# Row sums of squared differences: a new last piece, an early end of the tile context, and another assignment of blocks to partitions

## The chip, the core and the metric

The kernel runs on one core of a Trainium2 chip. A core has five engines that run side by side: TensorE (PE), VectorE (DVE), ScalarE (ACT), GpSimd (POOL) and SyncE (SP), and sixteen DMA engines that move data between the device's memory (HBM) and the core's memory (SBUF, 128 partitions). The metric is the device time of one execution in microseconds (us), lower is better. The time before is the median of nine runs.

## What is computed

```python
batch, dim = 1024, 4096
x = np.random.randn(batch, dim).astype(np.float32)
y = np.random.randn(batch, dim).astype(np.float32)

def reference(x, y, axis):          # axis = -1
    return np.sum((x - y) ** 2, axis=axis).astype(np.float32)
```

Two inputs of 16.8 MB are read once, and 1024 floats are written. There is nothing to reuse, and no matrix product.

## The kernel before

The 1024 rows are cut into 128 blocks of eight consecutive rows, one block to a partition: partition p holds rows 8p to 8p+7, a run of N = 8 x 4096 = 32768 columns. So every step of the kernel is about a range of columns of that run, in all 128 partitions at once. D is 4096, the length of a row; "row r" below means the r-th row of every block.

The run is loaded in pieces, listed by their widths in `xw` and `yw` (lines 78 and 79), large ones first and small ones at the end. A piece of x goes to the buffer X, one of y to Y. Both buffers hold H = 6 D columns, so the last two rows of a block come to lie where rows 0 and 1 lay. The y piece of 736 columns that ends row 3 is left out of its place (`late`, lines 80 to 82) and loaded second to last, and the last 352 columns of row 7 come last (line 94). The order is worked out from `ys`: each y piece is preceded by the x pieces that it needs (lines 117 to 123). All loads and the store are issued by SyncE, on one queue; each load has a semaphore of its own, which reaches 16 when it has landed.

The first two loads are put ahead of the barrier with which every program starts (`prog.early`, line 128); the next two, which fill the buffers, follow. The rest waits until squares of row 0 and row 1 are done (lines 223 to 230), because it overwrites these rows.

For each y piece, in the order of `ys`, VectorE waits for the load (`wait_loaded`), and subtracts in place, in parts that end at row ends (`sub`, line 172). ScalarE waits for the difference, squares it and sums it up along the columns into one number per partition (`square`, line 178). A row that has one part only gets its sum in `results` at once; a row in several parts has its partial sums in `parts`. There are three such rows. Row 6 is added up by VectorE (lines 231 to 241). Row 3 is completed by ScalarE, which adds its two partial sums with an Identity activation (lines 216 to 222). Row 7 ends on VectorE: it adds the partial sums so far into `head` (line 196), and one fused instruction (line 202) squares the last 352 differences, sums them and adds `head`.

SyncE then waits for both engines and stores the 128 x 8 results (lines 243 to 246), and waits for the store. `Program` writes all this into the program's first block, ahead of its branch, and takes the tile context's own bookkeeping off meanwhile (lines 16 to 22 and 42 to 50). The tile context closes at the end of the `with` statement in the launching code (line 278 of the profile): a barrier of all engines, GpSimd's clearing of the semaphores, and another barrier.

Of the kernel before, what the change touches and what calls it, by code (L numbers as in the profile page):

```python
# [8 lines left out]
class Program:  # L9
# [4 lines left out]


    def __init__(self, nc, tc):
        self.nc, self.hook = nc, tc.instruction_hook
        self.here = nc.cur_bb.bb.instructions
        self.entry = nc.main_func.blocks[0].instructions
        nc.remove_inst_callback(self.hook)  # L20
        self.lower, nc._always_lower_symbolic_ap = nc._always_lower_symbolic_ap, False
        self.before = len(self.here)

    def _take(self):
        taken = self.here[self.before :]
        del self.here[self.before :]
        return taken

    def _put(self, where):
        self.entry[where:where] = self._take()  # L30

    def early(self, engine):

        self._put(
            next(
                n
                for n, i in enumerate(self.entry)
                if i.engine == engine and str(i.opcode) == "Drain"
            )
        )  # L40

    def close(self):

        self._put(
            next(
                n for n, i in enumerate(self.entry) if str(i.opcode) == "UnconditionalBranch"
            )
        )
        self.nc._always_lower_symbolic_ap = self.lower
        self.nc.push_inst_callback(self.hook)  # L50


def kernel(tc, x, y, axis, out):
    nc = tc.nc
    P = nc.NUM_PARTITIONS
    F32 = mybir.dt.float32
    Square = mybir.ActivationFunctionType.Square
    Identity = mybir.ActivationFunctionType.Identity
    mult, add = mybir.AluOpType.mult, mybir.AluOpType.add

    B, D = x.shape
    R = B // P
    N = R * D


    xv = x.rearrange("(p r) d -> p (r d)", p=P)
    yv = y.rearrange("(p r) d -> p (r d)", p=P)
    ov = out.rearrange("(p r) -> p r", p=P)


    H = 6 * D
# [2 lines left out]
    results = nc.alloc_sbuf_tensor("results", [P, R], F32).ap()  # L74

    xw = [16384, 8192, 3072, 2688, 1312, 768, 352]
    yw = [15648, 8192, 3072, 2688, 1312, 768]
    late, last = 736, 352  # L80
    LATE = 3
    cut = (LATE + 1) * D - late
    assert sum(xw) == N and sum(yw) == N - late - last
# [4 lines left out]
    ys, c = [], 0  # L88
    for w in yw:
        ys.append((c, c + w))  # L90
        c += w
        if c == cut:
            c += late
    ys += [(cut, cut + late), (N - last, N)]

    diffs = tc.alloc_semaphore("diffs")
    acts = tc.alloc_semaphore("acts")
    sums = tc.alloc_semaphore("sums")
    stored = tc.alloc_semaphore("stored")
    n = dict(diffs=0, acts=0, sums=0)  # L100

    prog = Program(nc, tc)

    def home(c0, c1):
        h0 = c0 % H
        return slice(h0, h0 + c1 - c0)
# [3 lines left out]
    freed = []  # L110

    def load(landed, src, dst, name, c0, c1):
        sem = tc.alloc_semaphore("%s%d" % (name, len(landed)))
        nc.sync.dma_start(out=dst[:, home(c0, c1)], in_=src[:, c0:c1]).then_inc(sem, 16)  # L114
        landed.append(((c0, c1), sem))

    order = []
# [8 lines left out]
    for _ in range(2):  # L126
        load(*todo.pop(0))
    prog.early(mybir.EngineType.SP)
    while todo and todo[0][5] <= H:
        load(*todo.pop(0))  # L130


    row_parts = [[] for _ in range(R)]
    for c0, c1 in ys:
        while c0 < c1:
            e = min(c1, (c0 // D + 1) * D)
            row_parts[c0 // D].append((c0, e))
            c0 = e
    parts, where = None, {}
    total = sum(len(p) for p in row_parts if len(p) > 1)  # L140
    parts = nc.alloc_sbuf_tensor("parts", [P, total], F32).ap()
    head = nc.alloc_sbuf_tensor("head", [P, 1], F32).ap()
    k = 0
    for r, p in enumerate(row_parts):
        for piece in p:
# [2 lines left out]
    first = {}  # L148
# [6 lines left out]
    def parts_of(r, m):  # L155
        return parts[:, first[r] : first[r] + m]
# [3 lines left out]
    def wait_loaded(c1, ysem):  # L160

        waits = []
        while seen_x[0] < len(xs) and xs[seen_x[0]][0] < c1:
            waits.append(seen_x[0])
            seen_x[0] += 1
        nc.vector.wait_ge(ysem, 16)
        for k in waits:
            nc.vector.wait_ge(landed_x[k][1], 16)

    def sub(c0, c1):  # L170
        a = X[:, home(c0, c1)]
        nc.vector.tensor_sub(out=a, in0=a, in1=Y[:, home(c0, c1)]).then_inc(diffs, 1)  # L172
        n["diffs"] += 1

    def square(c0, c1, acc):
        a = X[:, home(c0, c1)]
        nc.scalar.wait_ge(diffs, n["diffs"])
        nc.scalar.activation(out=a, in_=a, func=Square, accum_out=acc).then_inc(acts, 1)  # L178
        n["acts"] += 1

    squared = {}
    reuse = []
    for j, (c0, c1) in enumerate(ys):
        final, tail = j == len(ys) - 1, j == len(ys) - 2
        wait_loaded(c1, landed_y[j][1])
        pieces = []
        while c0 < c1:
            e = min(c1, (c0 // D + 1) * D)
            pieces.append((c0, e))
            c0 = e  # L190
        for piece in pieces:
            sub(*piece)
            r = piece[0] // D
            if final:
                nc.vector.wait_ge(acts, squared[row_parts[r][-2]])
                nc.vector.tensor_reduce(  # L196
                    out=head, in_=parts_of(r, len(row_parts[r]) - 1), axis=mybir.AxisListType.X, op=add
                ).then_inc(sums, 1)
                n["sums"] += 1
                nc.vector.wait_ge(sums, n["sums"])  # L200
                nc.vector.wait_ge(diffs, n["diffs"])
                nc.vector.tensor_tensor_reduce(  # L202
                    out=Y[:, home(*piece)],
                    in0=X[:, home(*piece)],
                    in1=X[:, home(*piece)],
                    scale=1.0,
                    scalar=head,
                    op0=mult,
                    op1=add,
                    accum_out=results[:, r : r + 1],  # L210
                ).then_inc(sums, 1)
                n["sums"] += 1
                continue
            square(*piece, where[piece])
            squared[piece] = n["acts"]
            if tail:
                a, b = parts_of(r, 1), parts[:, first[r] + 1 : first[r] + 2]
                nc.scalar.wait_ge(acts, n["acts"])
                nc.scalar.activation(  # L219
                    out=results[:, r : r + 1], in_=b, func=Identity, bias=a  # L220
                ).then_inc(acts, 1)
                n["acts"] += 1
            if r in (0, 1):

                nc.sync.wait_ge(acts, n["acts"])
                while todo and todo[0][5] <= H + (r + 1) * D:
                    load(*todo.pop(0))
                if r == 1:
                    while todo:
                        load(*todo.pop(0))  # L230
        if j == len(ys) - 4:

            r = 6
            nc.vector.wait_ge(acts, squared[row_parts[r][-1]])
            nc.vector.tensor_reduce(  # L235
                out=results[:, r : r + 1],
                in_=parts_of(r, len(row_parts[r])),
                axis=mybir.AxisListType.X,
                op=add,
            ).then_inc(sums, 1)  # L240
            n["sums"] += 1

    nc.sync.wait_ge(sums, n["sums"])
    nc.sync.wait_ge(acts, n["acts"])
    nc.sync.dma_start(out=ov, in_=results).then_inc(stored, 16)
    nc.sync.wait_ge(stored, 16)
    prog.close()


# [33 lines left out]
```

## Time and profile before

| What | us |
|---|---|
| Median of nine runs | 86.02 |
| Their lowest and highest | 85.86, 86.43 |
| The profiled execution's own time | 86.43 |
| Its span, from the first to the last instruction of the kernel | 84.6 |
| VectorE busy | 36.3 (43%) |
| ScalarE busy | 31.7 (37%) |
| GpSimd busy | 0.2 |
| DMA: data moved, mean rate | 33.56 MB, 397 GB/s |
| First subtraction starts | 40.46 |
| Store issued | 82.26 |

The span is what the profile's times count in, from 0; the execution's own time also has what the runtime does around the kernel. VectorE and ScalarE are idle until 40.46, because the first pieces, half of all columns, land together. The row of busy tenths of the DMA engines, with 40 slices for the span, has nines and eights nearly throughout up to slice 38, and nothing in the last slice: what is at the end is not loading.

### The profile page before, as it was taken

Reading aid. Unit: us, or ns where it says so; the run is one execution under the profiler, and the core shown is the slowest. Engines: PE = TensorE matmul, PEld = TensorE weight load, DVE = VectorE, ACT = ScalarE, POOL = GpSimd, SP = SyncE. Lnnn points to the kernel's source line nnn. Section 1 sums busy time; section 2 is a strip of 40 time slices with the busy share of each in tenths; the row PEclk is TensorE's granted clock in tenths of the full one; section 3 lists DMA queues with packets and bytes.
Section 4 is the critical chain, followed back from the end, with each engine's and each line's share of the span. In section 5 each row is a group of like instructions: output and inputs, shape, how many; then the busy total and the mean of one; then the engine's idle time right before and its main releaser. Section 6 shows DMA issues by size and latency. Waiting matters only on the chain.

```text
span 84.6 us, 110 instructions
## 1 busy us (share of the span) xinstructions
DVE 36.3 (43%) x17; ACT 31.7 (37%) x26; POOL 0.2 (0%) x4
## 2 busy tenths in 40 slices
DVE  0000000000000000000899999990699999099870
ACT  4100000000000000000007979799404979996980
POOL 0000000000000000000000000000000000000000
DMA  9559999996699999995988997997999999999800
GB/s 496 248 248 496 496 496 496 496 465 268 266 444 473 473 473 473 473 473 248 480 372 387 496 480 325 434 480 298 412 430 412 431 432 437 402 417 411 323 1 2
DMA packets 2304, 33.56 MB, mean 397 GB/s; under 512 B 384, under 2 KB 640, under 8 KB 1280
## 3 DMA queue, kind: packets, MB, share of 16 engines
q1 hardware_dynamic: 2304, 33.56, 93.9%
HBM read 33.55 MB, written 0.00 MB: 396 GB/s over the span
## 4 chain that ended last, share of the span: by engine, by line
DMA 72%; DVE 14%; ACT 10%; SPq 1%; issue 0%
DMA Y<-in_y_dram 72%; DVE X L172 14%; ACT X L178 10%; SPq L114 1%; ACT results L219 0%
## 5 line engine op out<-in xcount | busy, mean ns | idle before, releaser
L172 DVE TENSOR_TENSOR X<-X,Y 128x4096 f32<-128x4096 f32 (+8 forms) x13 | 35.6, 2781 | 45.8 <-DMA Y<-in_y_dram 45.8
L178 ACT ACTIVATE X<-X 128x4096 f32<-128x4096 f32 (+7 forms) x12 | 29.4, 2452 | 49.2 <-DVE X L172 49.2
L178 ACT ACTIVATION_READ_ACCUMULATOR X<-X 128x1 f32 x12 | 2.2, 187 | 0.0
L178 ACT ACT_TABLE_LOAD x1 | 1.3, 1283 | 1.3 <-PEq L264 1.3
L202 DVE CUSTOM_DVE_ANT_0 Y<-X,head 128x352 f32<-128x352 f32 x1 | 0.6, 584 | 0.1
L219 ACT ACTIVATE results<-parts 128x1 f32<-128x1 f32 x1 | 0.3, 294 | 0.0
L196 DVE TENSOR_REDUCE head<-parts 128x1 f32<-128x3 f32 x1 | 0.1, 150 | 0.0
L235 DVE TENSOR_REDUCE results<-parts 128x1 f32<-128x2 f32 x1 | 0.1, 147 | 0.0
L264 POOL MEMSET const-bfloat16-1.0<- 128x1 bf16 x1 | 0.1, 102 | 0.0
L264 POOL MEMSET const-uint8-127<- 128x1 uint8 x1 | 0.1, 102 | 0.0
L264 POOL MEMSET const-float32-0.0<- 128x1 f32 x1 | 0.1, 99 | 0.2 <-issue 0.2
L264 POOL MEMSET const-float32-1.0<- 128x1 f32 x1 | 0.1, 99 | 0.0
L202 DVE DVE_READ_ACCUMULATOR2_ANT results<- 128x1 f32 x1 | 0.1, 82 | 0.0
## 6 DMA issues: line engine op xcount, KB each, us to landing
Y<-in_y_dram SPq DMA_DIRECT2D x1, 7824.0 KB, 40.0
X<-in_x_dram SPq DMA_DIRECT2D x1, 4096.0 KB, 48.9
Y<-in_y_dram SPq DMA_DIRECT2D x1, 4096.0 KB, 58.4
X<-in_x_dram SPq DMA_DIRECT2D x1, 1536.0 KB, 15.2
Y<-in_y_dram SPq DMA_DIRECT2D x1, 1536.0 KB, 18.5
X<-in_x_dram SPq DMA_DIRECT2D x1, 1344.0 KB, 17.8
Y<-in_y_dram SPq DMA_DIRECT2D x1, 1344.0 KB, 20.6
X<-in_x_dram SPq DMA_DIRECT2D x1, 656.0 KB, 21.8
```

What stands on the lines that cost most here:

```text
L114: nc.sync.dma_start(out=dst[:, home(c0, c1)], in_=src[:, c0:c1]).then_inc(sem, 16)
L172: nc.vector.tensor_sub(out=a, in0=a, in1=Y[:, home(c0, c1)]).then_inc(diffs, 1)
L178: nc.scalar.activation(out=a, in_=a, func=Square, accum_out=acc).then_inc(acts, 1)
L196: nc.vector.tensor_reduce(out=head, in_=parts_of(r, len(row_parts[r]) - 1), axis=mybir.AxisListType.X, op=add).then_inc(sums, 1)
L202: nc.vector.tensor_tensor_reduce(out=Y[:, home(*piece)], in0=X[:, home(*piece)], in1=X[:, home(*piece)], scale=1.0, scalar=head, op0=mult, ...
L219: nc.scalar.activation(out=results[:, r : r + 1], in_=b, func=Identity, bias=a).then_inc(acts, 1)
L235: nc.vector.tensor_reduce(out=results[:, r : r + 1], in_=parts_of(r, len(row_parts[r])), axis=mybir.AxisListType.X, op=add,).then_inc(sums, 1)
L264: nc = _bacc.Bacc("TRN2", target_bir_lowering=False, num_devices=1)
```

## The change

It has three parts.

The pieces. The widths are others. The late piece of row 3 of y is 160 columns in place of 736 and now comes last of all; the last piece of row 7 is 288 columns and comes second to last. So the fused instruction now completes row 3, with that row's one earlier partial sum, and row 7 is summed up behind it by `complete(7)`, as row 6 is by `complete(6)`. The `head` sum and the Identity activation are gone. There are 6 pieces of x in place of 7, and 9 of y in place of 8. A piece of x can now span two pieces of y.

The tile context. It is closed and compiled at the beginning of `Program.__init__`, so that its barriers stand ahead of the body. The body, but for the first two loads, stands behind the branch and behind these barriers. Behind the body GpSimd waits for the store and clears the semaphores, and no engine waits for another.

The blocks. Partition 8e+i takes block 16i+e, in x, in y and in the result. In memory the source is a pattern of 16 x 8 blocks; partitions 8e to 8e+7 hold blocks e, 16+e, 32+e and so on, each 2 MB behind the one before.

```diff
     def __init__(self, nc, tc):
-        self.nc, self.hook = nc, tc.instruction_hook
+        self.nc = nc
+        tc.close()
+        tc.compile()
         self.here = nc.cur_bb.bb.instructions
         self.entry = nc.main_func.blocks[0].instructions
-        nc.remove_inst_callback(self.hook)
-        self.lower, nc._always_lower_symbolic_ap = nc._always_lower_symbolic_ap, False
         self.before = len(self.here)
...
-    def close(self):
-
-        self._put(
-            next(
-                n for n, i in enumerate(self.entry) if str(i.opcode) == "UnconditionalBranch"
-            )
-        )
-        self.nc._always_lower_symbolic_ap = self.lower
-        self.nc.push_inst_callback(self.hook)
+    def close(self, sem, value):
+
+        self.nc.gpsimd.wait_ge(sem, value)
+        self.nc.clear_and_free_semaphores(self.sems)
...
-    xv = x.rearrange("(p r) d -> p (r d)", p=P)
-    yv = y.rearrange("(p r) d -> p (r d)", p=P)
-    ov = out.rearrange("(p r) -> p r", p=P)
+    G = 8
+    xv = x.rearrange("(i e r) d -> e i (r d)", i=G, r=R)
+    yv = y.rearrange("(i e r) d -> e i (r d)", i=G, r=R)
+    ov = out.rearrange("(i e r) -> e i r", i=G, r=R)
...
-    xw = [16384, 8192, 3072, 2688, 1312, 768, 352]
-    yw = [15648, 8192, 3072, 2688, 1312, 768]
-    late, last = 736, 352
+    xw = [16384, 8192, 5568, 1824, 512, 288]
+    yw = [16224, 8192, 2656, 2912, 928, 896, 512]
+    late, last = 160, 288
...
-    ys += [(cut, cut + late), (N - last, N)]
+    ys += [(N - last, N), (cut, cut + late)]
...
+    def complete(r):
+        nc.vector.wait_ge(acts, squared[row_parts[r][-1]])
+        nc.vector.tensor_reduce(
+            out=results[:, r : r + 1],
+            in_=parts_of(r, len(row_parts[r])),
+            axis=mybir.AxisListType.X,
+            op=add,
+        ).then_inc(sums, 1)
+        n["sums"] += 1
...
             if final:
-                nc.vector.wait_ge(acts, squared[row_parts[r][-2]])
-                nc.vector.tensor_reduce(
-                    out=head, in_=parts_of(r, len(row_parts[r]) - 1), axis=mybir.AxisListType.X, op=add
-                ).then_inc(sums, 1)
-                n["sums"] += 1
-                nc.vector.wait_ge(sums, n["sums"])
                 nc.vector.wait_ge(diffs, n["diffs"])
                 nc.vector.tensor_tensor_reduce(
...
-                    scalar=head,
+                    scalar=parts_of(r, 1),
...
-            if tail:
-                a, b = parts_of(r, 1), parts[:, first[r] + 1 : first[r] + 2]
-                nc.scalar.wait_ge(acts, n["acts"])
-                nc.scalar.activation(
-                    out=results[:, r : r + 1], in_=b, func=Identity, bias=a
-                ).then_inc(acts, 1)
-                n["acts"] += 1
...
+        if j == 4:
+            complete(6)
+    complete(7)
 
     nc.sync.wait_ge(sums, n["sums"])
-    nc.sync.wait_ge(acts, n["acts"])
     nc.sync.dma_start(out=ov, in_=results).then_inc(stored, 16)
-    nc.sync.wait_ge(stored, 16)
-    prog.close()
+    prog.close(stored, 16)
```

More of the change, by code (lines that the diff above doesn't have):

```diff
@@ L16, in __init__, with semaphore, early @@
     def __init__(self, nc, tc):
-        self.nc, self.hook = nc, tc.instruction_hook
+        self.nc = nc
+        tc.close()
+        tc.compile()
         self.here = nc.cur_bb.bb.instructions
         self.entry = nc.main_func.blocks[0].instructions
-        nc.remove_inst_callback(self.hook)
-        self.lower, nc._always_lower_symbolic_ap = nc._always_lower_symbolic_ap, False
         self.before = len(self.here)
-    def _take(self):
+        self.sems = []
+    def semaphore(self, name):
+        self.sems.append(self.nc.alloc_semaphore(name))
+        return self.sems[-1]
+    def early(self, engine):
         taken = self.here[self.before :]
         del self.here[self.before :]
[L27 to L32, printed above, removed]
-        self._put(
-            next(
-                n
-                for n, i in enumerate(self.entry)
-                if i.engine == engine and str(i.opcode) == "Drain"
-            )
-        )
-    def close(self):
-        self._put(
-            next(
-                n for n, i in enumerate(self.entry) if str(i.opcode) == "UnconditionalBranch"
-            )
-        )
-        self.nc._always_lower_symbolic_ap = self.lower
-        self.nc.push_inst_callback(self.hook)
+        where = next(
+            n
+            for n, i in enumerate(self.entry)
+            if i.engine == engine and str(i.opcode) == "Drain"
+        )
+        self.entry[where:where] = taken
+    def close(self, sem, value):
+        self.nc.gpsimd.wait_ge(sem, value)
+        self.nc.clear_and_free_semaphores(self.sems)
 def kernel(tc, x, y, axis, out):
@@ L57 @@
     Square = mybir.ActivationFunctionType.Square
-    Identity = mybir.ActivationFunctionType.Identity
     mult, add = mybir.AluOpType.mult, mybir.AluOpType.add
@@ L93 @@
             c += late
-    ys += [(cut, cut + late), (N - last, N)]
[L96 to L99, printed above, removed]
+    ys += [(N - last, N), (cut, cut + late)]
+    prog = Program(nc, tc)
+    diffs = prog.semaphore("diffs")
+    acts = prog.semaphore("acts")
+    sums = prog.semaphore("sums")
+    stored = prog.semaphore("stored")
     n = dict(diffs=0, acts=0, sums=0)
-    prog = Program(nc, tc)
     def home(c0, c1):
@@ L112, in load @@
     def load(landed, src, dst, name, c0, c1):
-        sem = tc.alloc_semaphore("%s%d" % (name, len(landed)))
-        nc.sync.dma_start(out=dst[:, home(c0, c1)], in_=src[:, c0:c1]).then_inc(sem, 16)
+        sem = prog.semaphore("%s%d" % (name, len(landed)))
+        nc.sync.dma_start(out=dst[:, home(c0, c1)], in_=src[:, :, c0:c1]).then_inc(sem, 16)
         landed.append(((c0, c1), sem))
@@ L141 @@
     parts = nc.alloc_sbuf_tensor("parts", [P, total], F32).ap()
-    head = nc.alloc_sbuf_tensor("head", [P, 1], F32).ap()
     k = 0
@@ L181 @@
     squared = {}
-    reuse = []
+    def complete(r):
[7 more added lines that the diff above has]
+        n["sums"] += 1
     for j, (c0, c1) in enumerate(ys):
-        final, tail = j == len(ys) - 1, j == len(ys) - 2
+        final = j == len(ys) - 1
         wait_loaded(c1, landed_y[j][1])
@@ L230 @@
                         load(*todo.pop(0))
[L231 to L241, printed above, removed]
+        if j == 4:
+            complete(6)
+    complete(7)
     nc.sync.wait_ge(sums, n["sums"])
-    nc.sync.wait_ge(acts, n["acts"])
     nc.sync.dma_start(out=ov, in_=results).then_inc(stored, 16)
-    nc.sync.wait_ge(stored, 16)
-    prog.close()
+    prog.close(stored, 16)
 _INS = ['x', 'y', 'axis']
```

## The prediction

> **What bounds the kernel now.** I read the chain that ended last first, then the stretches by time, then the last 10 us instruction by instruction, then the rows of the kernel's last line. The page's chain:
>
> ```profile
> DMA 72%; DVE 14%; ACT 10%; SPq 1%; issue 0%
> DMA Y<-in_y_dram 72%; DVE X L172 14%; ACT X L178 10%; SPq L114 1%; ACT results L219 0%
> ```
>
> Loading takes 72% of the span. Is the loading at a limit? The answer by stretches (columns: stretch, its length, busy us of VectorE, ScalarE, GpSimd, clock, DMA share, GB/s):
>
> ```profile
> 22.00:40.40 18.40, 0.00 (x0) 0.00 (x0) 0.00 (x0) 1.00 0.95 409
> 40.40:50.20 9.80, 9.74 (x3) 4.66 (x3) 0.00 (x0) 1.00 0.99 428
> 50.20:60.10 9.90, 6.93 (x3) 9.27 (x6) 0.00 (x0) 1.00 0.98 410
> 60.10:67.50 7.40, 7.40 (x2) 3.14 (x3) 0.00 (x0) 1.00 1.01 430
> ```
>
> The engines are busy 95 to 101% from start to end; a slice's GB/s jumps with packets that are counted whole, so the rate is better had from landings, in the page's list of issues:
>
> ```profile
> Y<-in_y_dram SPq DMA_DIRECT2D x1, 7824.0 KB, 40.0
> X<-in_x_dram SPq DMA_DIRECT2D x1, 4096.0 KB, 48.9
> X<-in_x_dram SPq DMA_DIRECT2D x1, 22.0
> ```
>
> The first x piece (64 KB in each of 128 partitions, 8.39 MB) lands at 22.0; y's first, issued at 0.42, at 40.4: 7824 KB in 18.4 us is 435 GB/s. At that rate 8.39 MB need 19.3 us, so 2.7 us of the first 22.0 are start-up. The last y piece is issued at 61.88 and lands 19.0 later, at 80.88. All 33.55 MB at 435 are 77.1 us, so 1.1 us are lost in the rest. From the last landing on, loading no longer counts:
>
> ```profile
> 77.08 1.68 ACT X L178 x2
> 78.76 0.00 issue
> 78.77 3.09 ACT X L178 x6
> 81.86 0.02 issue
> 81.88 0.29 ACT results L219
> ```
>
> This is the end of the chain in order of time: ScalarE squares without a gap from 77.08, ends 1.0 us behind the last landing, and the store is issued at 82.26. It lands 1.4 later, at 83.67. What comes then is 0.93 us up to 84.6, and the rows of the last line show it (operation, count, duration, first and last start):
>
> ```profile
> L278 POOLq EVENT_SEMAPHORE  x4: 17/17/17, 83.9 to 84.5; - x4
> L278 POOLq DRAIN  x3: 34/41/88, 1.2 to 84.4; - x3
> L278 SPq EVENT_SEMAPHORE  x2: 17/17/17, 84.1 to 84.6; - x2
> L278 SPq COMPARE_BRANCH  x1: 33/33/33, 83.7 to 83.7; - x1
> L278 POOLq EVENT_SEMAPHORE_RANGE_CLEAR  x1: 138/138/138, 84.2 to 84.2; - x1
> ```
>
> SyncE sees the store (83.7), a barrier of all engines runs (83.9 to 84.1), GpSimd clears the semaphores (84.2), and a second barrier runs (84.5 to 84.6). So the bounds, in order: 80.9 us of loading, 1.4 of tail, 1.4 of store, 0.9 of closing.
>
> [...]
>
> **The change part by part.**
>
> *Closing.* Two barriers go from the end to the start. At the start they stand ahead of the second x and y pieces (issued at 1.26 and 1.64). The closing pass at the end costs about 0.4 us per barrier (83.9 to 84.1 plus drains; 84.2 to 84.6), so these issues come some 0.5 to 1 us later; their engines are busy with the first two pieces until 40.4, which hides it, and ScalarE's table load with them. At the end GpSimd alone waits for the store. Nothing is queued behind that wait but its drain and the clear[...]. Cost: wake-up about 0.05, drain 0.1 (the row has 34 to 88 ns), clear 0.14, so 0.28 in place of 0.93: minus 0.65. Bounds: minus 0.9[...]; minus 0.3, if GpSimd's way out is slow.
>
> *Loads.* 15 before (7 x, 8 y), 15 after (6 x, 9 y), 128 packets each, the same bytes: the fixed costs per transfer cancel. y's first piece grows by 576 columns, 0.68 us at 435 GB/s, so subtraction starts at 41.1, and the second square, which now releases all later loads (x's third piece reaches into row 1's place), ends at 53.65 in place of 52.97. The queue holds work until 60.04 + 0.68, so 7 us of cover; eleven issues at 0.33 to 0.44 us are under 5 us. [...]an issue waits (3.1 us, in before), which was harmless 16 us ahead of the need and still is some 9 ahead. Cost 0.
>
> *Tail.* The rows by shape give VectorE 4420 ns for 4096 and 526 for 352 columns, so 1.04 ns a column + 0.16; ScalarE 3617 for 4096 and 817 for 736, 0.833 + 0.20. Before, 5600 columns remain behind y's fourth piece, which lands at 73.99: 6.89 us, 1.23 ns a column. After, 5408 remain: 6.65, so its counterpart (2912 wide) lands at 74.23. Subtractions of 1440 and 1472: 1.66 + 1.69, less 0.08 overlap, to 77.52. ScalarE is free by then (2656 from 73.6 takes 2.42, 1440 takes 1.40, to 77.45). From 77.55: 1472, 928, 896, 512, 288 at 1.43 + 0.98 + 0.95 + 0.63 + 0.44 = 4.43, to 81.98. Each of these is subtracted in time: 896 by 79.87 for 79.96, 512 by 80.7 for 80.9, 288 by 81.16 for 81.5. The accumulator's read adds 0.10, to 82.08. VectorE meanwhile: 160 subtracted by 81.39, the fused square-and-sum (584 ns for 352, so 0.38) and its read to 81.86; it is done first. Then row 7's reduction, 0.15 and two wake-ups of 0.03: store issue at 82.29, against 82.26. So the shorter last piece is worth nothing, as ScalarE sets the end: the Identity step (0.29) is replaced by wake-up and reduction. I take 0; bounds minus 0.25 and plus 0.3, since ScalarE's chain hangs on y's fourth piece within 0.1 us.
>
> *Store.* 128 pieces of 32 B as before[...] it took 1.4 with neighbours. I take 1.4; bounds minus 0.1, plus 0.3.
>
> *Block order.* Same packets, same partitions; what differs is which 128 KB block each engine reads at one moment[...]. [...] Bound below: start-up down from 2.7 by 0.5, and the stretch at 410 GB/s raised to 428 (0.4 us): minus 0.9. Above: see the slow rival. I take 0.
>
> Sum: minus 0.65. Against the profiled execution, 86.43 - 0.65 = 85.78; that one was the slowest of nine runs, 0.41 above their median, and the parts do not hang on it, so against the median 86.02 - 0.65 = 85.37.
>
> **Rivals.** (1) *The block order also helps*, at start-up and in the 50 to 60 us stretch: 85.37 - 0.9 = 84.5. For: 2.7 us of start-up, and a stretch of 410 with the same packets. Against: that stretch is also when SyncE issues eight loads, which stays. (2) *The closing saves nothing*: [...] 86.0. Against: the two barriers are serial work in the rows shown. (3) *Slower: the sixteen transfer engines collide in the new order*[...] in every load. If the rate of the slow stretch, 410 in place of the mean 420 (33.55 MB over 79.9 us), held throughout, loading would take 81.8, plus 1.9: 87.25. [...]half rate, plus some 75 us: 160. It decides from a loss of 0.65 us in 79.9, 0.8% of the rate. [...]
>
> **How the numbers follow.** Forecast 0.57, (1) 0.17, (2) 0.05, (3) 0.21. Forecast and (1) are faster: 0.74. (2) is the same within 0.2% (0.17 us, about what a measurement tells from no change): 0.05. (3) is slower: 0.21. The forecast's own range is 84.9 to 85.9 by the bounds of closing, tail and store; the range goes down to 84.4 for (1) and up to 87.0, which takes in the milder half of (3) and leaves its rest, about 0.12, and a little of (1) out.
>
> **What would show it.** Closing: the span ends 0.2 to 0.4 after the store's landing, with no barrier rows. Tail: ScalarE gapless from 77.5, the reduction of row 7 last before the store, issue at 82.2 to 82.4. Loads: last landing at 80.9 within 0.2, y's first at 41.1. Wrong, if the last landing moves by over 0.4 us either way (block order), or if the span shrinks by 0.65 and the time does not.

## The result, and the profile after

The changed kernel takes 165.67 us (median of ten runs, 164.14 to 166.38), against 86.02: 1.922 times as long, 95% interval 1.918 to 1.926. The profiled execution took 164.87, its span is 163.0, so 1.87 us lie outside the span, as the 1.83 before (86.43 less 84.6).

The page's parts 1, 3 and 4 of the changed kernel:

```profile
DVE 36.4 (22%) x18; ACT 32.2 (20%) x27; POOL 0.2 (0%) x4
...
q1 hardware_dynamic: 2304, 33.56, 97.2%
HBM read 33.55 MB, written 0.00 MB: 206 GB/s over the span
...
DMA X<-in_x_dram 27%; DMA Y<-in_y_dram 23%; SPq L110 16%; DVE X L167 6%; ACT X L173 2%; DVE Y L201 0%; DVE results L180 0%; DVEq L163 0%; SPq L217 0%; DVE results L201 0%
```

VectorE and ScalarE work about as long as before (36.3 and 31.7 us then). The packets (2304) are as many and the bytes the same. The DMA engines are busy 97.2% of a span that is nearly twice as long: they don't wait, each packet takes longer. One of 64 KB takes 5.11 us in the trace (the median of 128), where it took 2.42. In the chain a further quarter of the span has no name; by the stretches below it is loading too. The 16% at L110 are load issues of SyncE, the longest in the chain of 15.13 us (0.54 to 0.65 each for the first four). They are harmless, as those of 3.10 and 3.30 us were before: in the third stretch below, where they stand, the DMA engines are busy 99% of the time.

The page's list of issues (KB each, us from issue to landing):

```profile
Y<-in_y_dram SPq DMA_DIRECT2D x1, 8112.0 KB, 82.7
X<-in_x_dram SPq DMA_DIRECT2D x1, 4096.0 KB, 100.7
...
X<-in_x_dram SPq DMA_DIRECT2D x1, 43.4
out_dram<-results SPq DMA_DIRECT2D x1, 4.0 KB, 1.8
```

The first x piece (third row) lands at 43.4, where it took 22.0 before. The first y piece, issued at 0.69, lands at 83.4: 8.31 MB in 40.0 us are 208 GB/s, where it was 435. The answer by stretches, between these landings and the next ones, shows that nothing else has to run for this (stretch, its length, busy us of VectorE, ScalarE and GpSimd, clock, DMA share, GB/s):

```profile
43.40:83.40 40.00, 0.03 (x1) 0.00 (x0) 0.00 (x0) 1.00 0.94 195
83.40:103.30 19.90, 17.24 (x4) 13.76 (x7) 0.00 (x0) 1.00 1.01 211
103.30:123.30 20.00, 0.01 (x1) 0.95 (x2) 0.00 (x0) 1.00 0.99 207
```

With both compute engines all but idle (first and third row) or both busy (second), loading runs at half its former rate. It does so nearly to the end; only behind 150 us, where the pieces are small, does it rise, to 251 GB/s from 150 to 159 us. The closing did what was foreseen. The rows of GpSimd's last line:

```profile
L46 POOLq DRAIN  x1: 88/88/88, 162.8 to 162.8; - x1
L46 POOLq EVENT_SEMAPHORE_RANGE_CLEAR  x1: 138/138/138, 162.9 to 162.9; - x1
```

The store is issued at 160.93 and lands 1.8 later, at 162.7; the span ends 0.3 behind that, where it was 0.9.

### The profile page after: what moved, and what is told of

The parts are those of the page before. It is cut to its first block, busy times and chain, and to the rows that moved or that the text cites. A ratio compares the mean times of both kernels' runs of the same rounds, so it can differ in the third digit from the quotient of the medians.

```text
span 163.0 us, 109 instructions
## 1 busy us (share of the span) xinstructions
DVE 36.4 (22%) x18; ACT 32.2 (20%) x27; POOL 0.2 (0%) x4
## 2 busy tenths in 40 slices
DMA packets 2304, 33.56 MB, mean 206 GB/s; under 512 B 384, under 2 KB 768, under 8 KB 1408
## 3 DMA queue, kind: packets, MB, share of 16 engines
q1 hardware_dynamic: 2304, 33.56, 97.2%
## 4 chain that ended last, share of the span: by engine, by line
DMA 50%; another core or an unknown queue 25%; SPq 16%; DVE 6%; ACT 2%; issue 0%; DVEq 0%
DMA X<-in_x_dram 27%; DMA Y<-in_y_dram 23%; SPq L110 16%; DVE X L167 6%; ACT X L173 2%; DVE Y L201 0%; DVE results L180 0%; DVEq L163 0%; SPq L217 0%; DVE results L201 0%
## 5 line engine op out<-in xcount | busy, mean ns | idle before, releaser
L167 DVE TENSOR_TENSOR X<-X,Y 128x4096 f32<-128x4096 f32 (+9 forms) x14 | 35.8, 2594 | 124.5 <-DMA Y<-in_y_dram 124.3
L173 ACT ACTIVATE X<-X 128x4096 f32<-128x4096 f32 (+8 forms) x13 | 29.8, 2292 | 125.9 <-DVE X L167 125.8
```

## The experiments

### Is it the blocks? Taken out, and alone

`old_blocks` is the changed kernel with the assignment of before:

```diff
-    xv = x.rearrange("(i e r) d -> e i (r d)", i=G, r=R)
+    xv = x.rearrange("(p r) d -> p (r d)", p=P)
```

and so for y and the result; the index in the load follows. Two theories of the loss are put to the test from here on: H seeks it in the addresses that are read in HBM, P in the partitions that are written side by side in SBUF.

> The changed kernel with the assignment of blocks of before: partition p holds block p, source pattern 128 rows. Everything else as changed. Theory P[...] and theory H (HBM: sixteen engines that read blocks 128 KB apart collide in HBM) expect the same: the loss is gone, loading ends at 80.9, the closing gain of 0.65 us stays, 85.4 us (85.0 to 85.8).

Measured: 85.32 us (85.22 to 85.43), ratio to before 0.992 (0.991 to 0.994). This version is faster than both kernels. `blocks_alone` is the reverse, the kernel of before with these lines of the change alone.

> The kernel of before with the new assignment of blocks alone (partition 8e+i takes block 16i+e). P and H expect the whole loss: 64 KB packets at some 5.1 us, 165 to 167 us. If it were under 160, part of the loss would come from the new pieces or the closing.

Measured: 162.05, one execution, 3 us under what was expected. Without the assignment the whole loss is gone, and by itself it brings 76 us of it. Why the complete change is 3.6 us slower than that is open.

### HBM or SBUF: patterns in which the two part

The change alters two things at once: which addresses a load reads side by side, and into entries of how many partitions its pattern is divided. `blocks_64x2` and, later, `blocks_32x4` use the same formula with other factors, each in one execution. In 64 x 2 each eight partitions read 512 KB behind the eight before them, in 16 x 8 128 KB. Shown against `blocks_alone`:

```diff
-    G = 8
+    G = 2        # blocks_32x4: 4
```

> The kernel of before with a source pattern of 64 x 2 blocks: partition 2e+i takes block 64i+e. [...] P: 160 to 170 us, as with 16 x 8. H: 86 to 90 us.

Measured: 87.19. `lead128_pitch` keeps 128 partitions as the leading dimension and moves the addresses:

```diff
-    xv = x.rearrange("(p r) d -> p (r d)", p=P)
+    J = 4
...
+    xv = x.rearrange("(j p r) d -> p j (r d)", j=J, p=P)
```

and so for y and the result; a load that crosses a quarter becomes two.

> The kernel of before with a source pattern of 128 rows, in which neighbouring partitions are 32 KB apart (each partition takes two rows from each quarter of the batch), so that partitions four apart,[...] are 128 KB apart in HBM. Two loads are cut in two at the quarters, and the store is in pieces of 8 B. P: 86 to 88.5 us, loading at 420 GB/s or more. H: over 120 us.

Measured: 88.05, the store landing 3.3 us after its issue in place of 1.4. So H failed its own test. P failed in the form in which I had put it: it foresaw 160 to 170 for 64 x 2, which runs at full rate. Two narrower theories were left: P2, that the loss needs entries of eight partitions, and H2, that it needs sixteen streams inside 2 MB. `lead16_step7` has the form 16 x 8 at other addresses; it reads 113 of the 128 blocks, 15 of them twice (not 16, as the text below has it), so its sums are not those of the reference:

```diff
-        nc.sync.dma_start(out=dst[:, home(c0, c1)], in_=src[:, c0:c1]).then_inc(sem, 16)
+        nc.sync.dma_start(
+            out=dst[:, home(c0, c1)],
+            in_=bass.AP(src.tensor, c0, [[7 * N, 16], [N, 8], [1, c1 - c0]]),
+        ).then_inc(sem, 16)
```

> The kernel of before with a source pattern of 16 x 8 whose outer step is 7 blocks and whose inner step is 1 block: partition 8e+i takes block 7e+i. This leaves 16 blocks out and reads others twice; the bytes moved are the same. Sixteen streams are then 896 KB apart, much as in the kernel of before. Theory P2[...]: 160 us or more. Theory H2 (HBM: sixteen streams inside one window of 2 MB collide; neither 64 x 2 nor the 128-row pattern had that): 86 to 88 us.

Measured: 165.69, as slow as the change, with entries 896 KB apart in place of 128.

> The kernel of before with a source pattern of 32 x 4: partition 4e+i takes block 32i+e. P2[...]: 87 us. [...] H2: the streams lie 128 or 256 KB apart in windows of 1 to 4 MB, so anything from 87 to 160 us.

Measured: 86.72. Here are the issues of these two for the first y piece, with the same size, `lead16_step7` first:

```profile
Y<-in_y_dram SPq DMA_DIRECT2D x1, 7824.0 KB, 81.8
```

```profile
Y<-in_y_dram SPq DMA_DIRECT2D x1, 7824.0 KB, 39.9
```

The form of the pattern decides, not the addresses: 16 entries of 8 partitions are slow at either spacing, 32 of 4 and 64 of 2 are fast, with 128 KB from entry to entry as in the change. H2 is out.

### How many engines move how much

Under P2 my estimate was that four engines, on 32 partitions at a time, carry as much as eight on 64: a quarter of 435 GB/s is 109, and four engines at 64 KB in 2.42 us each are 108. Loads were cut into halves or quarters of the partitions, with the pattern 8 x 8 or 4 x 8 in each part:

```diff
+        for q in range(Q):     # half_8x8: Q = 2, quarter_4x8: Q = 4
+            nc.sync.dma_start(
+                out=dst[q * P // Q : (q + 1) * P // Q, home(c0, c1)],
+                in_=src[q, :, :, c0:c1],
+            ).then_inc(sem, 16)
```

> The kernel of before with each load cut into two halves of 64 partitions, each with a source pattern of 8 x 8, so that eight engines work[...]. P2: [...]109 GB/s: 64 KB packets at 5.1 us, loading 308 us, 310 to 325 us in all. H2: at half the demand there are no collisions, 64 KB packets at 2.42 us, loading 155 us, 160 to 175 us in all.

> Each load cut into four quarters of 32 partitions with a source pattern of 4 x 8, so that four engines work[...]. P2: 64 KB packets at 2.42 us, four times 27 GB/s, loading 309 us, 310 to 330 us in all: no longer than with eight engines in the halves. If instead each engine is slow by itself in such a pattern: packets at 5.1 us, 620 us.

Measured: 308.27, just under the range of P2, and 322.40, one execution each. The queue's line and the rate below it on the two pages, `half_8x8` first (packets, MB, share of 16 engines):

```profile
q1 hardware_dynamic: 2304, 33.56, 49.1%
HBM read 33.55 MB, written 0.00 MB: 109 GB/s over the span
```

```profile
q1 hardware_dynamic: 2304, 33.56, 24.5%
HBM read 33.55 MB, written 0.00 MB: 105 GB/s over the span
```

The share says that eight engines (half of sixteen) were busy throughout in the one, and four in the other, with the same number of packets of the same sizes. Eight engines moved 109 GB/s, four 105. So four of them, on 32 partitions at a time, run at 26 GB/s each, and eight on 64 at 14, about half of that. It is no matter of an engine being slow in such a pattern, and none of what HBM gives, which was 435 before.

### The destination alone

`step4_2x8` and `step8_2x8` differ in the destination partitions only. A load has two entries of eight partitions; the second entry lies 32 partitions behind the first in `step4_2x8`, 64 in `step8_2x8`. Two engines work (the DMA share is 0.12 to 0.13, two of sixteen):

```diff
     def mine(q):
-        return slice(q, q + 121, 8)                                        # step8_2x8
+        return slice(q // 4 * 64 + q % 4, q // 4 * 64 + q % 4 + 61, 4)     # step4_2x8
```

> The kernel of before with each load cut into eight of 16 partitions, source pattern 2 x 8, so that two engines work[...] (the 16 partitions lie four apart). Source addresses are those of the run beside it, step8_2x8; only the destination partitions differ. [...]27 GB/s, loading 1230 us or more. If it isn't a matter of the destination: as step8_2x8.

> As step4_2x8, with the same source addresses, but the 16 partitions of a load lie eight apart[...]. [...]54 GB/s, loading 617 us, 620 to 680 us in all, half of step4_2x8. If it isn't a matter of the destination: the same time as step4_2x8.

Measured: 658.98 and 635.08, one execution each. The second is as expected; the first is not the 1230 that I had worked out. The stretches from the start (the last two figures are DMA share and GB/s), `step4_2x8` first:

```profile
0.00:40.00 40.00, 0.00 (x0) 0.00 (x0) 0.20 (x4) 1.00 0.12 29
40.00:80.00 40.00, 0.00 (x0) 0.00 (x0) 0.00 (x0) 1.00 0.13 48
80.00:120.00 40.00, 0.00 (x0) 0.00 (x0) 0.00 (x0) 1.00 0.12 52
120.00:160.00 40.00, 0.00 (x0) 0.21 (x1) 0.00 (x0) 1.00 0.13 56
```

```profile
0.00:40.00 40.00, 0.00 (x0) 0.00 (x0) 0.20 (x4) 1.00 0.12 52
40.00:80.00 40.00, 0.00 (x0) 0.00 (x0) 0.00 (x0) 1.00 0.13 56
80.00:120.00 40.00, 0.00 (x0) 0.00 (x0) 0.00 (x0) 1.00 0.12 52
```

With entries 32 partitions apart, two engines begin at 29 GB/s, about the rate of one (26 in `quarter_4x8`), busy all the time; with entries 64 apart, they begin at 52. So the destination alone costs them about half of their rate. But the loss dissolves: in the next stretches the first run moves 48, 52 and 56 GB/s, the rates of the second.

With the pattern 8 x 8 it lasts. The rows of GB/s in 40 slices, `half_8x8` first, then `quarter_4x8`:

```profile
GB/s 137 68 137 68 137 68 137 68 137 86 117 131 65 131 82 114 131 65 131 98 97 103 107 103 103 124 103 111 107 103 101 117 119 120 118 123 123 145 192 55
```

```profile
GB/s 98 98 98 131 98 98 131 98 98 129 94 102 117 94 125 94 125 94 125 98 98 115 115 98 115 102 110 115 100 104 110 104 109 107 103 106 107 104 102 20
```

For three quarters of the time eight engines move no more than four do (106 and 107 GB/s, the means of the first 30 slices); in the last full slice, where the pieces are small, they move 192 against 102. In the change itself the rise to 251 comes too late to matter. Why the loss ends early in `step4_2x8` and late in the others was not shown.

### The other two parts of the change

`closing_alone` is the kernel of before with the new `Program` and its `close`; `pieces_alone` has the new widths, the new order and `complete(7)`.

> The kernel of before with the new closing alone: tile context closed at the beginning, GpSimd waits for the store and clears. By the sum of the prediction minus 0.65: 85.4 us (85.1 to 85.7). [...]

> The kernel of before with the new pieces and the new order of the end alone. By the sum of the prediction 0 (minus 0.25 to plus 0.3): 86.0 us (85.8 to 86.3). If the shorter last piece counts in full, the tail is shorter by some 0.2 to 0.3: 85.7.

Measured: 85.46 (85.38 to 85.53), ratio 0.993 (0.9917 to 0.9944), that is 0.60 us less (0.48 to 0.71); and 85.94 (85.80 to 86.14), ratio 0.9982 (0.9970 to 0.9993), 0.15 us less (0.06 to 0.26). Together 0.75, against 0.67 (0.55 to 0.78) in `old_blocks`, where both are made. Each is below 1% of the time, but clear of no change.

## Why the prediction was wrong, point by point

**The step that failed** is the one headed block order: "Same packets, same partitions; what differs is which 128 KB block each engine reads at one moment", with "I take 0". The packets and the partitions of the whole load are the same, but not the form of the pattern: a source of 128 rows, or of entries of two or four partitions, loads at full rate (86.02, 87.19 and 86.72 us), one of 16 entries of eight partitions at half (208 GB/s), at either spacing of its addresses; and in the runs with two engines the choice of destination partitions alone takes the rate of the first 40 us from 52 to 29 GB/s. The term was not 0 but plus 80 us, from 85.32 to 165.67 (76 by `blocks_alone`).

The trace of before, with one pattern in it, could not decide this. But the price was worked out ("half rate, plus some 75 us: 160") and came within 6 us; it stood as the far end of rival (3), whose own time was given as 87.25, and the range left it out. A rival that doubles a bound needs a chance of its own; a mild version in front of it hid it.

**Steady state, 435 GB/s**: right for the old blocks. `old_blocks` loads its first y piece at 435 GB/s too (8.31 MB in 19.1 us).

**Closing, minus 0.65**: right; 0.60 alone. The rival in which the closing saves nothing, 86.0, has fallen: what lies outside the span is 1.86 us in `closing_alone` (85.46 less 83.6), as the 1.83 before, so the time fell with the span. The moved barriers delay the second x piece's issue from 1.26 to 1.91 in `old_blocks`, and nobody waits for it before 41.0.

**Loads, 0**: right where the blocks are the old ones: subtraction starts at 41.02 (foreseen 41.1), the square that releases the later loads ends at 53.53 (53.65).

**Tail, 0, within minus 0.25 and plus 0.3**: within its bounds, with a small gain of 0.15 in `pieces_alone`. The end of the chain in order of time, of `old_blocks`:

```profile
70.24 2.94 DVE X L166
73.18 0.02 issue
73.20 8.28 ACT X L172 x14
81.48 0.02 issue
81.50 0.16 DVE results L179
```

ScalarE works without a gap up to 81.48, and row 7's reduction comes last, as the sum had it; the store is issued at 81.69. The gap-free run begins at 73.20, earlier than the 77.5 that I named: the piece of 2656 columns is part of it. The chain hangs on y's third piece, then, not on its fourth.

The moments foreseen for the end were late even with the old blocks: the last landing was to come at 80.9 within 0.2 and the store at 82.2 to 82.4, and `old_blocks` has them at 80.3 and 81.69. The prediction had counted them from the profiled execution of before and said that the parts do not hang on its being 0.41 above the median. The moments do: in `closing_alone`, with the pieces and blocks of before, the last load also lands 0.4 earlier, at 80.5. So the prediction's sign of being wrong on the block order, a last landing moved by over 0.4, would have shown without any change of that order.

**Store, 1.4, bound plus 0.3**: too low; 1.8, just outside the bound. The distance of 512 B between the 32 B pieces of neighbouring partitions is not what counts: with 1 KB (`blocks_32x4`) and 2 KB (`blocks_64x2`) it is 1.8 too. What these stores share is a pattern that splits the partitions over two dimensions, e and i, with the columns as a third. The issue of such a transfer took longer as well: the first x piece's takes 0.38 us in `old_blocks` and 0.65 in the changed kernel, the store's 0.35 and 0.59. In `lead16_step7`, with the two-dimensional store of before, it lands 1.4 later again.

## What to carry to other kernels

When a transfer's pattern changes, try its form by itself, at other source addresses and other destination partitions, and do not stop at whether all sixteen engines are busy. Here 32 x 4 costs 0.7 us over 128 rows (one execution) and 16 x 8 costs 76. Busy DMA engines say nothing of their rate (97.2% at 206 GB/s, 93.9% at 397): divide the bytes of one load by the time between two landings. And give a rival whose price is a multiple of the gain its own line and its own chance.

## What the runs showed of the hardware that was not expected

- In runs that differ in the destination alone, two engines moved 29 GB/s in the first 40 us with entries 32 partitions apart, and 52 with entries 64 apart. The first rose to 48, 52 and 56 in the next three stretches of 40 us by itself. In `half_8x8` eight engines moved no more than four for some 230 of 306.5 us, and came to 192 GB/s only at the end.
- A pattern that splits the partitions over two dimensions made a transfer's issue some 0.16 to 0.27 us longer (`old_blocks` against the changed kernel), and the 4 KB store landed 0.4 us later (1.8 in place of 1.4).
- Sources 128 KB apart did no harm by themselves on a core that loads alone: `lead128_pitch`, in which partitions four apart read 128 KB apart, moved 435 GB/s between 22.0 and 40.4 us.
- Which engine writes which partition is not in the trace, so by what means the destination matters was not shown. Shown are the rates of 16, 8 and 4 engines in entries of eight partitions (208, 109 and 105 GB/s) and the pair of runs that differ in the destination alone.
